# A decoder step on one Trainium2 core: the first loads in smaller pieces for three q products, key pages held back, and every product's three passes 320, 256 and 288 columns wide

## The chip, the cores and the metric

The kernel runs on one core of a Trainium2 chip. The time is device microseconds (us) of one execution, as the median of several runs. The engines are TensorE (PE; its weight loads are listed as PEld), VectorE (DVE), ScalarE (ACT), GpSimd (POOL) and SyncE (SP), which issues most of the DMA transfers from one queue. A name with a q, such as SPq, is an engine's sequencer.

## The reference

One layer of a hybrid decoder is applied to 256 prompt positions and 8 x 4 sample positions. The two groups share all weights, so the kernel treats them as T = 288 columns.

```
h   = RMSNorm(x)                                   # x: 288 x 2048
q, k, v, u, v_g = split(h @ w_in)                  # 5 x 1024 columns
A   = MoBA attention(rope(q), rope(k), v)          # samples also read paged keys and values
B   = gelu(u) * (tril(W_s) @ LN(gelu(v_g)) + b)
mix = (sigmoid(h Wg_a) * (A Wa) + sigmoid(h Wg_b) * (B Wb)) @ w_o
x   = x + RMSNorm(mix)
x   = x + RMSNorm((silu(a1) * g1) @ w_ffn_out)     # a1, g1 = split(RMSNorm(x) @ w_ffn_in)
x   = x + (p @ w_ple) * sigmoid(RMSNorm(x) @ w_ple_gate)
```

The samples' past is 8 x 16 pages of keys and as many of values, 512 KB each, found through a page table. All data are fp32.

## The kernel before

Activations lie transposed, 128 features on the partitions and the 288 positions in a row; 2048 features are 16 such slices, numbered k. The work horse is `product` (L209 to L237): for 256 output columns (two accumulator tiles, t = 0 and 1, one PSUM bank each) it loads weights in pieces of four slices (512 KB, tile `wr`, L218, four buffers). It splits each piece into a rounded part `wh` (ACT, L224) and a remainder `wl` (DVE, L225), three buffers each. The activations have such parts too, side by side in one row of 2 x 288 columns (`hh`, `hl` of `hhl` for the first products; `mhl`, `zhl`, `dhl` later). Three matmuls per slice and tile add up: `wh` times the rounded part (L228), `wh` times the remainder (L229), `wl` times the rounded part (L230).

An argument `wide` shifts columns between the first two: with `wide=32`, L228 takes 320 columns, that is all 288 of the rounded part and the first 32 of the remainder, whose result goes to 32 extra accumulator columns. L229 takes the other 256. After the last slice ACT copies the extra columns out (`rest`, L234), DVE adds them to the first 32 (L235), and only then `done` reads the accumulators. Before the change only the product `f` (w_ffn_out) has `wide=32`; its remainder therefore joins its first pass.

There are 112 products of the other kinds: q, k, v, g and u (four each, from `w_in`), gb and ga (gates), b, a and o (eight each), fa and fg (22 each), pg (eight). Until the last `ga` there are three accumulator banks in pool `acc` (two in `long`, three in `aux`), so a product's second tile takes a bank that the product before it still has to free. From `a` on there are six.

The program's start: ACT issues the load of the gains, SP that of x in four pieces of four slices (576 KB) and the weights of two q products, q0 in `acc` and q1 in `long`. `h_parts` makes `hh` and `hl` of a piece, `squares` its share of the row norm, `r0_of` the factor `r0` from a matmul with ones (`r0p`). Ten matmuls on a constant (`wake`, L168; the trace lists each fp32 matmul of this kind twice) run before any data are there. The constants `cst`, `kcst` (POOL) and `cm` (ACT) are loaded at once, and `page_load` (L554) issues key pages as soon as the table is there, twelve until the buffers are full. A `done` of q multiplies by `r0` and applies the rotation `rope`, which reads `cm`. Then follow k, v, the rest of the first half with the pages' work between the products (`weave`), and from `a` on products alone.

A scheduler with a model of the chip orders the instructions of each engine. `tc.issue_after(i)` tells it that what follows stands after i; on i's own engine that is an order without a wait. SP's DMA transfers go through one queue, and in the trace they land in the order of issue. The transfers of SP and ACT take eight completion semaphores in turn and wait for the one before on theirs, so that at most eight are under way.

Of the kernel before, what the change touches and what calls it, by code (L numbers as in the profile page):

```python
# [19 lines left out]
KD = D // 128  # L20
# [19 lines left out]
GC = 256  # L40

QUADS = NPG // 4
WAKE, WR, BIG, PT, AUX, PB, LEAD, EG, LE, N1, N2, REST = 10, 4, 3, 1, 3, 2, 6, 2, 4, 20, 38, 325.0

# [64 lines left out]
def tile_hybrid_step(ctx: ExitStack, tc: tile.TileContext, a: dict, o: list):  # L109
    nc = tc.nc  # L110
# [34 lines left out]
    ident = cst
# [39 lines left out]

    def h_parts(c):
        for i in range(XK):
            k = c * XK + i
            nc.scalar.activation(hh[:, k], xs[c][:, i], AF.Copy, scale=g_pre[:, k:k + 1])
            nc.vector.scalar_tensor_tensor(hl[:, k], xs[c][:, i], g_pre[:, k:k + 1], hh[:, k], op0=ALU.mult, op1=ALU.subtract)  # L190
# [9 lines left out]
    def r0_of():  # L200
# [5 lines left out]
        rstd_of(r0, r0p, p_x0.tile([128, T], F32, name="r0t"))  # L206


    def product(w, c0, ks, part, done, name, of="acc", wide=0, hold=()):  # L209


        accs = [bank([128, T + wide], f"{name}{t}", of) for t in range(2)]
        n = len(ks)
        for k0 in range(0, n, 4):
            m = min(4, n - k0)
            raw = perm.tile([128, 4, GC], F32, name="wr", bufs=WR)
            r0 = ks[k0] * 128
            nc.sync.dma_start(raw[:, :m], w[r0:r0 + m * 128, c0:c0 + GC].rearrange("(k p) c -> p k c", p=128))  # L218
            wh = perm.tile([128, 4, GC], F32R, name="wh", bufs=3)
# [742 lines left out]
    for half in range(2):  # L962
# [118 lines left out]
```

## Time and profile before

| | |
|---|---|
| three runs | 1820.21, 1820.64 (median), 1822.02 us |
| the profiled execution, its own time | 1820.68 us |
| its span, first to last instruction | 1818.9 us (1.78 us lie around it) |
| PE busy | 1798.5 us, 99% |
| DVE, ACT, POOL busy | 951.9, 769.2, 90.6 us |
| mean granted PE clock | 0.996 of 2.4 GHz |
| HBM read, written | 407.45 MB, 4.85 MB |

PE is busy nearly all the time, but its ends are modelled: matmuls overlap, one starts about 132 ns after the other and is listed with 295 ns. So the time of a stretch of products is read from the starts: its length divided by the number of matmuls in it.

### The profile page before, as it was taken

Reading aid. Unit: us, or ns where it says so; the run is one execution under the profiler, and the core shown is the slowest. Engines: PE = TensorE matmul, PEld = TensorE weight load, DVE = VectorE, ACT = ScalarE, POOL = GpSimd, SP = SyncE. Lnnn points to the kernel's source line nnn. Section 1 sums busy time; section 2 is a strip of 40 time slices with the busy share of each in tenths; the row PEclk is TensorE's granted clock in tenths of the full one; section 3 lists DMA queues with packets and bytes.
Section 4 is the critical chain, followed back from the end, with each engine's and each line's share of the span. In section 5 each row is a group of like instructions: output and inputs, shape, how many; then the busy total and the mean of one; then the engine's idle time right before and its main releaser. Section 6 shows DMA issues by size and latency. Waiting matters only on the chain.

```text
span 1818.9 us, 38387 instructions
## 1 busy us (share of the span) xinstructions
PE 1798.5 (99%) x15818; PEld 1752.1 (96%) x15818; DVE 951.9 (52%) x1363; ACT 769.2 (42%) x1081; POOL 90.6 (5%) x169
## 2 busy tenths in 40 slices
PE   7999999999999999999999999999999999999998
PEld 7999899999999989999999999999999999999998
DVE  6654447544344346544854555434455554444774
ACT  5334465444333344445533333333333333444642
POOL 1010112000000000011000000000000000011000
PEclk9999999999999999999999999999999999999999
DMA  9589999999999995555555555455555555546363
GB/s 345 163 280 367 323 360 337 365 350 359 352 345 368 358 321 201 170 164 161 152 169 166 163 167 169 157 168 165 172 165 172 163 164 170 165 158 195 122 196 112
DMA packets 309136, 414.81 MB, mean 228 GB/s; under 512 B 13120, under 2 KB 273344, under 8 KB 308832
## 3 DMA queue, kind: packets, MB, share of 16 engines
q1 hardware_dynamic: 307728, 409.16, 67.0%
q8 instruction: 124, 2.03, 0.5%
q0 software_dynamic: 944, 2.79, 0.4%
q10 hardware_dynamic: 288, 0.41, 0.1%
q14 instruction: 52, 0.43, 0.1%
HBM read 407.45 MB, written 4.85 MB: 227 GB/s over the span
## 4 chain that ended last, share of the span: by engine, by line
PE 94%; DVE 3%; DMA 1%; SPq 1%; issue 1%; ACT 1%; DVEq 0%; ACTq 0%
PE f L228 6%; PE f L230 5%; PE fg L228 5%; PE fg L230 5%; PE fg L229 5%; PE fa L230 5%; PE fa L228 5%; PE fa L229 5%; PE f L229 5%; PE values L696 3%; PE scores L598 3%; PE gb L228 2%; PE ga L228 2%; PE gb L230 2%; PE o L228 2%; PE o L230 2%
## 5 line engine op out<-in xcount | busy, mean ns | idle before, releaser
L225 DVE TENSOR_TENSOR wl<-wr,wh 128x1024 fp32r<-128x1024 f32 x512 | 618.8, 1209 | 708.2 <-ACT wh L224 704.4
L224 ACT CAST wh<-wr 128x1024 fp32r<-128x1024 f32 x512 | 530.9, 1038 | 881.0 <-PE f L229 140.4
L228 PE MATMUL f<-dhl,wh 128*128 128x320 f32 x704 | 217.1, 308 | 0.0
L229 PE MATMUL fg<-zhl,wh 128*128 128x288 f32 x704 | 208.2, 296 | 0.0
L230 PE MATMUL fa<-zhl,wl 128*128 128x288 f32 x704 | 206.8, 295 | 1.2 <-DVE wl L225 1.2
L229 PE MATMUL fa<-zhl,wh 128*128 128x288 f32 x704 | 207.9, 296 | 0.0
L228 PE MATMUL fg<-zhl,wh 128*128 128x288 f32 x704 | 207.3, 295 | 0.2 <-ACT wh L224 0.2
L230 PE MATMUL fg<-zhl,wl 128*128 128x288 f32 x704 | 207.0, 295 | 0.0
L230 PE MATMUL f<-dhl,wl 128*128 128x288 f32 x704 | 207.0, 294 | 0.0
L228 PE MATMUL fa<-zhl,wh 128*128 128x288 f32 x704 | 206.3, 296 | 0.1
L229 PE MATMUL f<-dhl,wh 128*128 128x256 f32 x704 | 196.6, 279 | 0.0
L230 PEld LDWEIGHTS fa<-zhl,wl 128*128 128x128 f32 x704 | 133.3, 189 | 1.4 <-DVE wl L225 1.4
L230 PEld LDWEIGHTS fg<-zhl,wl 128*128 128x128 f32 x704 | 133.3, 190 | 0.0
L229 PEld LDWEIGHTS f<-dhl,wh 128*128 128x128 f32 x704 | 132.4, 188 | 0.0
L228 PEld LDWEIGHTS fg<-zhl,wh 128*128 128x128 f32 x704 | 132.1, 188 | 0.4 <-ACT wh L224 0.4
L229 PEld LDWEIGHTS fa<-zhl,wh 128*128 128x128 f32 x704 | 132.4, 188 | 0.1
L229 PEld LDWEIGHTS fg<-zhl,wh 128*128 128x128 f32 x704 | 132.3, 188 | 0.0
L228 PEld LDWEIGHTS fa<-zhl,wh 128*128 128x128 f32 x704 | 131.6, 188 | 0.7 <-ACT zhl L937 0.4
L230 PEld LDWEIGHTS f<-dhl,wl 128*128 128x128 f32 x704 | 132.2, 188 | 0.0
L228 PEld LDWEIGHTS f<-dhl,wh 128*128 128x128 f32 x704 | 132.0, 188 | 0.0
L228 PE MATMUL gb<-hhl,wh 128*128 128x288 f32 x256 | 76.7, 300 | 0.0
L228 PE MATMUL ga<-hhl,wh 128*128 128x288 f32 x256 | 76.5, 299 | 0.0
(327 smaller groups left out, 3740.6 us busy)
## 6 DMA issues: line engine op xcount, KB each, us to landing
wr<-in_w_ffn_in SPq DMA_DIRECT2D x176, 512.0 KB, 3.7
kt<-in_cache_k SPq DMA_DIRECT2D x128, 512.0 KB, 7.7
vt<-in_cache_v SPq DMA_DIRECT2D x128, 512.0 KB, 6.6
wr<-in_w_in SPq DMA_DIRECT2D x80, 512.0 KB, 7.2
wr<-in_w_ffn_out SPq DMA_DIRECT2D x80, 512.0 KB, 3.4
wr<-in_w_gate SPq DMA_DIRECT2D x64, 512.0 KB, 7.4
wr<-in_w_o SPq DMA_DIRECT2D x32, 512.0 KB, 3.5
wr<-in_w_ple_gate SPq DMA_DIRECT2D x32, 512.0 KB, 3.5
```

The source lines that it names most:

```text
L224: nc.scalar.copy(wh[:, :m], raw[:, :m])
L225: nc.vector.tensor_tensor(wl[:, :m], raw[:, :m], wh[:, :m], ALU.subtract)
L228: nc.tensor.matmul(accs[t], wh[:, i, c], x[:, :T + wide], start=k == 0, stop=False)
L229: nc.tensor.matmul(accs[t][:, wide:T], wh[:, i, c], x[:, T + wide:], start=False, stop=False)
L230: late["mm"] = nc.tensor.matmul(accs[t][:, :T], wl[:, i, c], x[:, :T], start=False, stop=k == n - 1)
L598: i = nc.tensor.matmul(sp[b][32 * g:32 * g + 32, 4 * n:4 * n + 4], Q[:, h2, g, dq], kt[:, :, c:c + 32], start=h2 == 1 and dq == 0, stop=h2 ...
L696: i = nc.tensor.matmul(oa[b][32 * g:32 * g + 8], w[:, n, 32 * g + 8 * part:32 * g + 8 * part + 8], v[:, :, g], start=first and part == 3, ...
```

## The change

Seven things change. (1) x comes in six pieces: slice 0, slice 1 (issued by ACT), slices 2 and 3, and then three pieces of four slices. (2) Three q products, not two, work on each piece (the third in `aux`), and the weights that meet the small pieces are loaded in pieces of the same slices: six loads of 128 KB, three of 256 KB, and 512 KB from there on. (3) The squares of the last piece and `r0_of` stand behind the matmuls of the second product's last piece. (4) `cst` and `kcst` go through SP behind the twelfth weight load, `cm` through SP behind the fourteenth. (5) The first twelve page loads each stand behind a weight load, the first behind the tenth. (6) `wake` has eight matmuls in place of ten. (7) `wide` is 32 for all products.

```diff
-WAKE, WR, ... = 10, 4, ...
+WAKE, FIRST, WR, ... = 8, 12, 4, ...
...
-    def x_load(c):
-        nc.sync.dma_start(xs[c], a["x"][:, c * XK:c * XK + XK])
+    pieces = [(0, 1), (1, 2), (2, 4)] + [(k, k + XK) for k in range(XK, KD, XK)]
+    def x_load(k0, k1):
+        (nc.scalar if k0 == 1 else nc.sync).dma_start(xs[k0 // XK][:, k0 % XK:k0 % XK + k1 - k0], a["x"][:, k0:k1])
...
-    x_load(0)
+    x_load(*pieces[0])
+    x_load(*pieces[1])
-    nc.gpsimd.dma_start(cst, a["c_perm"][:, :128])
-    nc.gpsimd.dma_start(kcst, a["c_perm"][:, 128:])
...
-    def product(w, c0, ks, part, done, name, of="acc", wide=0, hold=()):
+    def product(w, c0, ks, part, done, name, of="acc", wide=32, cuts=None, hold=()):
-        for k0 in range(0, n, 4):
-            m = min(4, n - k0)
-            raw = perm.tile([128, 4, GC], F32, name="wr", bufs=WR)
+        for k0, k1 in cuts or [(k, min(k + 4, n)) for k in range(0, n, 4)]:
+            m = k1 - k0
+            if cuts and m < 4:
+                raw = p_x0.tile([128, m, GC], F32, name=f"w{m}", bufs=6 // m)
+            else:
+                raw = perm.tile([128, 4, GC], F32, name="wr", bufs=WR)
-            nc.sync.dma_start(raw[:, :m], ...)
+            loads.append(nc.sync.dma_start(raw[:, :m], ...))
...
-    q2 = [q_gen(0), q_gen(1, "long")]
-    for c in range(KD // XK):
-        h_parts(c)
-        for q in q2:
-            next(q)
-        if c + 1 < KD // XK:
-            x_load(c + 1)
-        squares(c)
-    r0_of()
+    q3 = [q_gen(g, of, pieces) for g, of in enumerate(("acc", "long", "aux"))]
+    for i, (k0, k1) in enumerate(pieces):
+        h_parts(k0, k1)
+        for q in q3:
+            if k1 == KD and q is q3[2]:
+                squares(k1 // XK - 1)
+                with tc.issue_after(late["mm"].ins):
+                    r0_of()
+            next(q)
+        if 1 < i + 1 < len(pieces):
+            x_load(*pieces[i + 1])
+        if k1 % XK == 0 and k1 < KD:
+            squares(k1 // XK - 1)
+    with tc.issue_after(loads[11].ins):
+        nc.sync.dma_start(cst, a["c_perm"][:, :128])
+        nc.sync.dma_start(kcst, a["c_perm"][:, 128:])
-    nc.scalar.dma_start(cm, a["c_mix"])
+    with tc.issue_after(loads[13].ins):
+        nc.sync.dma_start(cm, a["c_mix"])
...
+            if len(issued) < FIRST:
+                st.enter_context(tc.issue_after(loads[9 + len(issued)].ins))
...
-    for q in q2 + [q_gen(2), q_gen(3)]:
+    for q in q3 + [q_gen(3)]:
```

The order of the built programs at three places. First PE at the program's start, before; q_116 and q_117 are the two accumulators of the first q product:

```order
L168 MATMUL wake<-ones_d 128x128 x10
L228 MATMUL q_116<-hhl,wh 128x288
L229 MATMUL q_116<-hhl,wh 128x288
L228 MATMUL q_117<-hhl,wh 128x288
L229 MATMUL q_117<-hhl,wh 128x288
L230 MATMUL q_116<-hhl,wl 128x288
L230 MATMUL q_117<-hhl,wl 128x288
```

The same place in the changed program, where q_107 and q_108 belong to the first product, q_121 and q_122 to the second, q_135 and q_136 to the third:

```order
L169 MATMUL wake<-ones_d 128x128 x8
L235 MATMUL q_107<-hhl,wh 128x320
L236 MATMUL q_107<-hhl,wh 128x256
L235 MATMUL q_108<-hhl,wh 128x320
L236 MATMUL q_108<-hhl,wh 128x256
L237 MATMUL q_107<-hhl,wl 128x288
L237 MATMUL q_108<-hhl,wl 128x288
L235 MATMUL q_121<-hhl,wh 128x320
L236 MATMUL q_121<-hhl,wh 128x256
L235 MATMUL q_122<-hhl,wh 128x320
L236 MATMUL q_122<-hhl,wh 128x256
L235 MATMUL q_135<-hhl,wh 128x320
```

The first pass now reads the remainder `hl` too, and after six matmuls on slice 0 the next product's weights for slice 0 are used, where before the first product went on with slices 1 to 3.

Second, SP's queue up to the first key page (`kt`), before:

```order
L137 DMA x_76<-in_x 128x1152
L218 DMA wr<-in_w_in 128x4x256 x2
L137 DMA x_77<-in_x 128x1152
L218 DMA wr<-in_w_in 128x4x256 x2
L137 DMA x_78<-in_x 128x1152
L137 DMA x_79<-in_x 128x1152
L559 TENSOR_LOAD pt_sb
L559 ISA x2
L560 ISA
L560 DMA kt<-in_cache_k 128x1024
L218 DMA wr<-in_w_in 128x4x256
```

In the changed program the queue begins with slice 0 of x, six weight loads of 128 KB, slices 2 and 3 of x and three weight loads of 256 KB. From the first piece of four slices on it reads:

```order
L139 DMA x_77<-in_x 128x1152
L225 DMA wr<-in_w_in 128x4x256 x3
L139 DMA x_78<-in_x 128x1152
L225 DMA wr<-in_w_in 128x4x256
L139 DMA x_79<-in_x 128x1152
L272 DMA cst<-in_c_perm 128x128
L273 DMA kcst<-in_c_perm 128x448
L576 TENSOR_LOAD pt_sb
L576 ISA x2
L577 ISA
L577 DMA kt<-in_cache_k 128x1024
```

Three more pages follow before the next weight load (the fourteenth), and from there on pages and weight loads take turns, one by one. Before, one to four pages stood between two weight loads.

Third, ACT at the program's end, before and after the change; pg_22755 and pg_22756 are the accumulators of the last product:

```order
L1019 ACTIVATE pgt<-pgt 128x288 x2
L224 CAST wh<-wr 128x1024
L1019 ACTIVATE pgt<-pgt 128x288 x2
L1077 UNCONDITIONAL_BRANCH
```

```order
L231 CAST wh<-wr 128x1024
L1036 ACTIVATE pgt<-pgt 128x288
L241 COPY rest<-pg_22755 128x32
L241 COPY rest<-pg_22756 128x32
L1036 ACTIVATE pgt<-pgt 128x288 x2
L1094 UNCONDITIONAL_BRANCH
```

Two copies of 32 columns now stand ahead of the last product's sigmoids, as they do at the end of every product. Where three banks are in use, PE's order mostly has 24 matmuls of a product's first tile ahead of the first of its second tile; before it mostly had 21.

## Rows read from the trace of the kernel before

**Rows 1.** The page, part 1: busy time, share and instructions of each engine.

```profile
PE 1798.5 (99%) x15818; PEld 1752.1 (96%) x15818; DVE 951.9 (52%) x1363; ACT 769.2 (42%) x1081; POOL 90.6 (5%) x169
```

**Rows 2.** Timeline of PE: start and duration (us), instruction, [idle time before it <-releaser].

```profile
1.07 4.63 PE L168 MATMUL wake<-ones_d 128*128 128x128 f32 x20 [1.07 <-DVE eps L160]
9.54 0.61 PE L228 MATMUL q<-hhl,wh 128*128 128x288 f32 x1 [3.84 <-ACT wh L224]
...
42.63 0.40 PE L228 MATMUL q<-hhl,wh 128*128 128x288 f32 x1 [2.50 <-ACT wh L224]
...
45.00 0.85 PE L230 MATMUL q<-hhl,wl 128*128 128x288 f32 x2 [1.58 <-DVE wl L225]
```

**Rows 3.** Busy time in stretches of the start; last: clock, DMA share, GB/s.

```profile
0.00:25.00 25.00, 20.10 (x123) 19.52 (x124) 16.86 (x27) 17.76 (x27) 5.70 (x16) 0.93 0.97 340
25.00:30.00 5.00, 5.00 (x37) 4.79 (x36) 3.22 (x5) 1.56 (x2) 0.00 (x0) 1.00 1.04 389
40.00:45.00 5.00, 0.92 (x5) 0.56 (x4) 4.92 (x10) 2.67 (x3) 0.00 (x0) 0.87 0.86 272
45.00:50.00 5.00, 5.00 (x21) 5.00 (x22) 2.89 (x3) 0.50 (x2) 0.00 (x0) 0.50 0.65 189
0.00:81.19 81.19, 71.16 (x474) 69.05 (x475) 53.42 (x76) 35.09 (x44) 6.43 (x19) 0.94 0.79 267
```

**Rows 4.** The chain that ended last, first 50 us: start, us, what.

```profile
1.21 7.21 DMA wr<-in_w_in
...
23.93 10.81 DMA wr<-in_w_in
...
45.85 0.24 PE q L228
```

**Rows 5.** Timeline of ACT in the same stretch.

```profile
5.52 1.81 ACT L189 ACTIVATE hhl<-x,gains 128x288 fp32r<-128x288 f32 x4 [2.83 <-DMA gains<-in_gains]
...
30.72 1.05 ACT L224 CAST wh<-wr 128x1024 fp32r<-128x1024 f32 x1 [1.66 <-DMA wr<-in_w_in]
```

**Rows 6.** Busy time in stretches: pages' phase, then a, o, fa with fg, f, pg.

```profile
200.00:300.00 100.00, 99.24 (x1190) 90.47 (x1190) 51.76 (x102) 51.91 (x90) 18.44 (x33) 1.00 1.02 366
696.79:748.05 51.26, 51.26 (x384) 51.26 (x385) 35.68 (x60) 22.06 (x32) 0.00 (x0) 1.00 0.64 218
748.05:849.65 101.60, 101.60 (x771) 101.60 (x770) 43.53 (x42) 47.59 (x69) 14.92 (x13) 1.00 0.56 180
899.11:1140.96 241.85, 241.85 (x1827) 241.85 (x1825) 123.42 (x153) 92.73 (x114) 0.00 (x0) 1.00 0.53 166
1140.96:1280.19 139.23, 139.23 (x1059) 139.23 (x1057) 56.70 (x66) 53.85 (x79) 0.00 (x0) 1.00 0.52 165
1738.87:1812.99 74.12, 74.12 (x561) 74.07 (x560) 43.33 (x68) 28.74 (x37) 0.00 (x0) 1.00 0.50 163
```

**Rows 7.** Groups by line and form on ACT and DVE: busy us, mean ns, idle before.

```profile
L224 ACT CAST wh<-wr 128x1024 fp32r<-128x1024 f32 x496 | 520.9, 1051 | 849.5 <-PE fg L229 136.5 <-PE fa L229 127.6 <-PE f L229 108.8
L189 ACT ACTIVATE hhl<-x,gains 128x288 fp32r<-128x288 f32 x16 | 7.2, 524 | 2.8 <-DMA gains<-in_gains 2.8
L234 ACT COPY rest<-f 128x32 f32<-128x32 f32 x32 | 5.6, 175 | 3.6 <-PE f L230 3.6
...
L225 DVE TENSOR_TENSOR wl<-wr,wh 128x1024 fp32r<-128x1024 f32 x496 | 607.7, 1226 | 685.7 <-ACT wh L224 681.9 <-DMA kt<-in_cache_k 3.2 <-PE values L696 0.2
L190 DVE SCALAR_TENSOR_TENSOR hhl<-x,gains,hhl 128x288 fp32r<-128x288 f32 x16 | 7.1, 515 | 0.0
L235 DVE TENSOR_TENSOR f<-f,rest 128x32 f32<-128x32 f32 x32 | 6.2, 193 | 2.1 <-ACT rest L234 2.0
```

**Rows 8.** Timeline of ACT and DVE behind the last `f` product's second tile.

```profile
1699.66 0.19 ACT L234 COPY rest<-f 128x32 f32<-128x32 f32 x1 [0.60 <-PE f L230]
...
1699.87 0.20 DVE L235 TENSOR_TENSOR f<-f,rest 128x32 f32<-128x32 f32 x1
...
1700.11 0.46 DVE L995 TENSOR_TENSOR fo<-fo,f 128x288 f32<-128x288 f32 x1
```

More of the change, by code (lines that the diff above doesn't have):

```diff
@@ L42 @@
 QUADS = NPG // 4
-WAKE, WR, BIG, PT, AUX, PB, LEAD, EG, LE, N1, N2, REST = 10, 4, 3, 1, 3, 2, 6, 2, 4, 20, 38, 325.0
+WAKE, FIRST, WR, BIG, PT, AUX, PB, LEAD, EG, LE, N1, N2, REST = 8, 12, 4, 3, 1, 3, 2, 6, 2, 4, 20, 38, 325.0
 C_ID, C_G, C_OWN, C_L = 0, 128, 256, 256 + TS * NB
@@ L184, in tile_hybrid_step, with h_parts @@
     hh, hl = hhl[:, :, :T], hhl[:, :, T:]
[L186 to L190, printed above, removed]
+    def h_parts(k0, k1):
+        for k in range(k0, k1):
+            x = xs[k // XK][:, k % XK]
+            nc.scalar.activation(hh[:, k], x, AF.Copy, scale=g_pre[:, k:k + 1])
+            nc.vector.scalar_tensor_tensor(hl[:, k], x, g_pre[:, k:k + 1], hh[:, k], op0=ALU.mult, op1=ALU.subtract)
     def squares(c):
@@ L206, in r0_of @@
         rstd_of(r0, r0p, p_x0.tile([128, T], F32, name="r0t"))
-    def product(w, c0, ks, part, done, name, of="acc", wide=0, hold=()):
+    loads = []
+    def product(w, c0, ks, part, done, name, of="acc", wide=32, cuts=None, hold=()):
         accs = [bank([128, T + wide], f"{name}{t}", of) for t in range(2)]
         n = len(ks)
-        for k0 in range(0, n, 4):
-            m = min(4, n - k0)
-            raw = perm.tile([128, 4, GC], F32, name="wr", bufs=WR)
+        for k0, k1 in cuts or [(k, min(k + 4, n)) for k in range(0, n, 4)]:
[4 more added lines that the diff above has]
+                raw = perm.tile([128, 4, GC], F32, name="wr", bufs=WR)
             r0 = ks[k0] * 128
-            nc.sync.dma_start(raw[:, :m], w[r0:r0 + m * 128, c0:c0 + GC].rearrange("(k p) c -> p k c", p=128))
+            loads.append(nc.sync.dma_start(raw[:, :m], w[r0:r0 + m * 128, c0:c0 + GC].rearrange("(k p) c -> p k c", p=128)))
             wh = perm.tile([128, 4, GC], F32R, name="wh", bufs=3)
@@ L245, in tile_hybrid_step, with q_gen @@
     w_gate = a["w_gate"].rearrange("l k c -> (l k) c")
-    def q_gen(g, of="acc"):
-        yield from product(w_in, g * GC, K16, hpart, lambda x: rope(qT[:, 2 * g:2 * g + 2], x), "q", of)
-    q2 = [q_gen(0), q_gen(1, "long")]
-    for c in range(KD // XK):
-        h_parts(c)
-        for q in q2:
-            next(q)
-        if c + 1 < KD // XK:
-            x_load(c + 1)
-        squares(c)
-    r0_of()
+    def q_gen(g, of="acc", cuts=None):
+        yield from product(w_in, g * GC, K16, hpart, lambda x: rope(qT[:, 2 * g:2 * g + 2], x), "q", of, cuts=cuts)
+    q3 = [q_gen(g, of, pieces) for g, of in enumerate(("acc", "long", "aux"))]
[6 more added lines that the diff above has]
+                    r0_of()
+            next(q)
+        if 1 < i + 1 < len(pieces):
[5 more added lines that the diff above has]
+        nc.sync.dma_start(kcst, a["c_perm"][:, 128:])
     end_x0.close()
@@ L1006, in tile_hybrid_step @@
                 le_weights(range(LE, 8))
-            drain(product(w_fo, g * GC, ks, lambda k: dhl[:, k], lambda x, g=g: fo_done(x, g), "f", wide=32))
+            drain(product(w_fo, g * GC, ks, lambda k: dhl[:, k], lambda x, g=g: fo_done(x, g), "f"))
     r4 = norm_gap("fo", range(LE, 8))
```

## The prediction, made before the result was known

> **What bounds the kernel now.** I read the page first: PE is busy 99% of the span [rows 1]. So time can come from two places only: stretches in which PE waits or runs at its lower clock, and the time that one matmul takes. The waits of PE were next, in time order: nearly all lie in the first 50 us [rows 2]. PE does nothing useful until 9.54, then stops at 42.63 (2.50 us) and 45.00 (1.58 us). The reader is to see in [rows 3] what goes with it: the granted clock is 0.93 over the first 25 us and 0.50 from 45 to 50, its lower level of 1.2 GHz; there matmuls start 0.24 us apart [rows 4] where 0.1326 is usual (below).
>
> What ends these waits is DMA. At the start the chain goes through the first weight load, 512 KB that land after 7.21 us at 8.42 [rows 4]; ACT had been ready since 5.52, when the gains landed [rows 5]. Later it goes through a load issued at 23.93 that takes 10.81 us, because key pages lie ahead of it in the queue [rows 4]. The queue itself is full: 340 GB/s over the first 25 us, 389 after [rows 3].
>
> How much the start loses: 81.19 us [rows 3] is a point at which PE has done the four q products (384 matmuls), the four of r0p and 66 of k: 454, the row's 474 less the 20 of wake. At 0.1326 us they are 60.2 us. The loss is 81.19 - 60.2 = 21.0 us.
>
> **The change, part by part.**
>
> *First matmul.* Three things must be there: the gains, slice 0 of x, the first 128 KB of weights. Before, 576 KB of x, 44 KB of gains and other transfers shared the first us, and the gains landed at 5.5. Now 44 + 144 + 128 KB and slice 1 (144 KB) lead. I take 5.0 for gains, x and weights (not earlier than 4.0, not later than 5.5, where the larger pieces had landed). Then ACT makes `hh` (0.52), DVE `hl` (0.52) [rows 7], on which the first pass now depends; the cast of 256 columns beside it is about a quarter of 1.05. First matmul: 6.0 instead of 9.54.
>
> *Work per byte.* For each slice of x three products have 18 matmuls, 2.4 us, for 528 KB of x and weights, about 1.5 us at the rates of [rows 3]. Before it was 12 matmuls per slice. So PE should not run dry in the first slices.
>
> *Clock.* Before, wake ended at 5.7 and PE then stood for 3.84 us [rows 2]; from 9.54 some 14 matmuls ran 0.24 us apart, 1.5 us lost, and from 45 some 23 more, 2.5 us. Now wake ends near 4.8 and work begins at 6.0. I keep 1.0 us of loss (0 to 1.5), and none later, since I see no wait of over a us ahead.
>
> *The fourteenth weight load* is the first behind pages: four of them. Up to its end the queue moves 8.99 MB (gains, all of x, 14 loads, `cst`, `kcst`, four pages). By [rows 3] 8.5 MB are moved at 25 us and the rest by 26.3. What lag follows, an old load shows: ACT starts on it at 30.72, released by DMA [rows 5], with 9.88 MB up to it; these rates give 28.5, so 2.2 us. The fourteenth load then lands near 28.5 and its cast (1.05) ends at 29.5. PE comes to it after 168 matmuls, at 6.0 + 22.3 + 1.0 = 29.3. I take a wait of 0.5 us (0 to 3). After it a load and a page are 1.05 MB, 2.7 us at 389 GB/s, and PE works 24 x 0.1326 = 3.18 us on a load, so the queue gains on PE. `cst`, `kcst` and `cm` add 0.66 MB that was moved before too; their place costs nothing beyond this sum.
>
> *r0 and rope.* Three products now wait for `r0` at once: six multiplications and three rotations on DVE, where there were four and two, among `wl` splits of 1.23 us [rows 7] that PE needs every 3.18 us. `cm` is issued late, behind a load that waits for its buffer, and may come later than `r0`. I add 0.7 us of PE waits (0 to 4).
>
> So the same work is done at 6.0 + 60.2 + 1.0 + 0.5 + 0.7 = 68.4 instead of 81.19: 12.8 us gained. The bounds are 8.5 (first matmul at 7.0, clock 1.5, waits of 2 and 2) and 14.5 (first matmul at 5.0, clock 0.5, waits 0.2 less).
>
> *Does the head start last?* Pages wait for buffers that PE's products free, so the whole later pattern moves along. Where the queue is fullest, 366 GB/s from 200 to 300, PE still works 99.24 of 100 us [rows 6], and 389 has been seen [rows 3].
>
> *The three widths.* Passes of 320, 256 and 288 columns stream 864, as three of 288 do. Whether it pays is read from the only product that has them [rows 6], length by matmuls (those that began before the stretch left out): f 139.23/1056 = 131.85 ns. The others: fa and fg 241.85/1824 = 132.60, pg 74.12/560 = 132.36, o 101.60/768 = 132.29, a 51.26/384 = 133.5. So f is the quickest by 0.4 to 0.75 ns (a apart), but products of one and the same form differ by as much. 9984 matmuls get the new widths: 4224 of fa and fg at 0.75, 768 of o at 0.44, 768 of pg at 0.5, and 4224 others at about 0.6 would give 6.4 us in all. The lower bound is a loss of 2, since operands alone move a matmul by a ns either way. I take 4.0, nearer to the row of f.
>
> The Trainium skill speaks against this gain: "TensorE: Matmul & The Clock Gate", in "Back-to-back issue gap", gives a start-to-start gap of the columns over the clock plus a fixed cost per matmul. By it three passes of equal sum cost the same, and this term is 0. The rows agree on columns and a fixed cost, though with some 12 ns where the page has 2.5; the 0.75 ns of f lie outside the rule.
>
> *Ends of products.* 112 products get two copies (0.175) and two additions (0.193) [rows 7], 39 us on ACT and 43 on DVE in all, on engines that are half idle [rows 1]. They count where nothing covers them. From the copy to the reader of the accumulator is 0.45 us for a tile [rows 8]. This lies bare at the kernel's end (+0.5) and ahead of the row norm behind o (+0.5); that behind f has it already. Elsewhere the next product's first tile covers it. Sum: +1.0, bounds 0.5 and 3.
>
> **Sum**: -12.8 - 4.0 + 1.0 = -15.8. The profiled execution took 1820.68, 0.04 above the median, so both give 1805.
>
> **The rivals.** What a measurement can tell from no change is some 0.2%, 3.6 us.
>
> (A) As summed: 1805, chance 0.53.
>
> (B) The widths give nothing, the start gives all of it: 1820.7 - 12.8 + 1.0 = 1809. For it: forms alike differ by as much as f does from them. Against: f is below each of them, and keeps it over 1056 matmuls. Chance 0.24. It is what the skill's rule would make of the change.
>
> (C) The start gives much less. Small pieces keep the queue emptier: with few transfers under way it moved 189 GB/s [rows 3]. Were the first 2.1 MB moved at this rate, not at 380, they would take 11.1 us, not 5.5; PE would run dry for 5.6 us and lose some 2.5 more at its lower clock, as from 45 us on: 1805 + 8 = 1813. Against it: six pieces are issued before anything has landed. Chance 0.10.
>
> (D) The head start is given back: if the queue sets the pace of the pages' phase, PE meets it there and waits 13 us longer, and the widths gain only behind it, about 2.5 us: 1820.7 - 2.5 + 1.0 = 1819, no change. Against: 99.24 of 100 us busy [rows 6]. Chance 0.05.
>
> (E) Slower: the three-bank boundaries. Some 41 products start while the product before still holds a bank. Its release now takes a copy, an addition and the reader, and the copy and the addition may each stand behind a cast (1.05) and a split (1.23) [rows 7]: with 0.45 for the reader some 3.1 us in all, against 24 matmuls or 3.18 us of cover. One more cast ahead would make PE wait about 0.6 us each: 41 x 0.6 = 25, so 1830. It decides from 15.8/41 = 0.39 us per product on. Against it: most orders leave 24 matmuls as cover. Chance 0.08.
>
> **The numbers.** Faster by over 0.2% are A, B and C, and a mild form of E: 0.88. Same 0.05, slower 0.07. The range goes from A with the start at its upper bound and the widths at theirs (1820.7 - 14.5 - 6.4 + 0.5 = 1800), widened by a us for what a shifted order may add, to C: 1799 to 1814. D and E lie outside.
>
> **What the profile would show.** Right: first product matmul near 6 us, no PE wait of over 1.5 us in the first 80, qrp and the first k products some 12 us earlier, lower clock nowhere behind 15 us; fa, fg, o, pg at about 131.9 ns per matmul; the pages' phase as busy as before; the end longer by half a us. Wrong: a first matmul later than 8, a wait at the fourteenth load (it would be released by ACT `wh` behind DMA), waits of L235 on bank releases by DVE between 80 and 700 us, pitches of 132.3 or more in fa, or key pages on the chain.

## The result

| | median (lowest to highest) | ratio to before, 95% interval |
|---|---|---|
| before | 1820.3 us (1818.87 to 1822.02, 5 runs) | |
| changed | 1800.88 us (1799.44 to 1801.96, 5 runs) | 0.9891, 0.9877 to 0.9906 |

The changed kernel is faster by 19.4 us, or 1.1%. Forecast were 1805 and 1799 to 1814. The profiled execution took 1801.96 us, of which the span is 1800.2. Direction and size came out; the two large terms of the sum did not. Their errors pull in opposite directions, so that the total comes this close is in part luck.

The page's first part, which answers to [rows 1]: PE is busy 15.0 us less than before.

```profile
PE 1783.5 (99%) x15814; PEld 1739.2 (97%) x15814; DVE 987.4 (55%) x1593; ACT 797.8 (44%) x1309; POOL 84.6 (5%) x167
```

The timeline of PE in the start, beside [rows 2]: start and duration in us, the instruction, in brackets the idle time before it and what ended it.

```profile
3.79 1.06 PE L169 MATMUL wake<-ones_d 128*128 128x128 f32 x4
4.59 0.61 PE L235 MATMUL q<-hhl,wh 128*128 128x320 f32 x1
...
10.46 0.41 PE L235 MATMUL q<-hhl,wh 128*128 128x320 f32 x1 [0.50 <-DVE hhl L191]
...
16.72 0.53 PE L237 MATMUL q<-hhl,wl 128*128 128x288 f32 x2 [0.46 <-DVE wl L232]
...
31.16 0.42 PE L235 MATMUL q<-hhl,wh 128*128 128x320 f32 x1 [2.04 <-ACT wh L231]
...
32.42 0.67 PE L237 MATMUL q<-hhl,wl 128*128 128x288 f32 x2 [0.47 <-DVE wl L232]
```

Windows of the start, beside [rows 3] (busy us of PE, PEld, DVE, ACT and POOL with counts; last the granted clock, the DMA share, GB/s). 71.68 is where the 66th k matmul starts; before, it started at 81.06, and was done 0.13 us later, at the 81.19 of [rows 3].

```profile
0.00:25.00 25.00, 22.98 (x154) 22.34 (x155) 17.23 (x32) 19.28 (x34) 4.55 (x14) 1.00 0.94 320
25.00:30.00 5.00, 4.12 (x32) 3.90 (x30) 4.25 (x6) 1.64 (x2) 0.00 (x0) 1.00 1.05 379
30.00:35.00 5.00, 3.38 (x15) 3.15 (x16) 2.30 (x2) 2.09 (x2) 0.00 (x0) 0.77 1.06 375
35.00:40.00 5.00, 5.00 (x36) 5.00 (x35) 1.90 (x3) 2.10 (x2) 0.00 (x0) 0.89 1.07 379
...
0.00:71.68 71.68, 67.15 (x469) 65.85 (x470) 51.40 (x85) 36.99 (x58) 4.55 (x14) 0.98 0.88 300
```

The reader is to see three things. The first product matmul now follows `wake` without a gap (4.59 for 9.54), and the first 25 us have a granted clock of 1.00. Then PE waits 2.04 us at 31.16, for the cast of the fourteenth weight load. Behind this wait the clock falls for the only time in the start: 0.77 and 0.89 over ten us, so 0.23 x 5 + 0.11 x 5 = 1.7 us are lost at the lower level, 1.2 GHz. The chain (start, us, what) shows the load behind it, beside [rows 4]:

```profile
21.16 8.82 DMA wr<-in_w_in
30.06 1.05 ACT wh L231
```

The products' stretches, beside [rows 6]: a, o, fa with fg, f, pg.

```profile
684.45:735.08 50.63, 50.63 (x387) 50.63 (x385) 39.59 (x76) 24.95 (x48) 0.00 (x0) 1.00 0.66 223
735.08:836.34 101.26, 101.26 (x771) 101.26 (x770) 46.00 (x58) 49.55 (x85) 13.95 (x13) 1.00 0.56 180
886.39:1125.53 239.14, 239.14 (x1826) 239.14 (x1825) 128.87 (x192) 97.79 (x153) 0.00 (x0) 1.00 0.54 168
1125.53:1264.77 139.24, 139.24 (x1058) 139.24 (x1057) 57.16 (x68) 53.85 (x80) 0.00 (x0) 1.00 0.52 165
1720.19:1793.74 73.55, 73.55 (x561) 73.46 (x560) 45.36 (x81) 30.69 (x52) 0.00 (x0) 1.00 0.51 164
```

Length by matmuls, as before: fa and fg 239.14/1824 = 131.11 ns (132.60), a 50.63/384 = 131.85 (133.5), o 101.26/768 = 131.85 (132.29), pg 73.55/560 = 131.3 (132.36), f 131.86 (131.85). So fa, fg and pg fell below f, which was the best row before.

Where the 18.7 us of span came from, by when the same matmul starts: 9.4 are gained at the 66th matmul of k, 12.3 at a's first, 13.3 behind o, 15.4 at f's first, 19.2 at the last of pg, 18.7 at the end. Two places give time back: the norms ahead of fa (1.35 us) and ahead of pg (0.56), where fa's and pg's first pass of 320 columns now needs 32 columns of the remainder `zl`, and the kernel's end (0.53). The first is seen in the waits of PE (us in total, times, longest):

```profile
PE q L235 <- ACT wh L231: 2.0, 1, 2.0
PE fa L235 <- DVE zhl L955: 1.5, 1, 1.5
PE pg L235 <- DVE zhl L955: 1.5, 1, 1.5
```

Before, pg waited 0.9 at this place for ACT's half of `zhl`.

### The profile page after: what moved, and what is told of

It is laid out like the page before. It is cut to its first block, busy times and chain, and to the rows that moved or that the text cites. A ratio compares the mean times of both kernels' runs of the same rounds, so it can differ in the third digit from the quotient of the medians.

```text
span 1800.2 us, 38851 instructions
## 1 busy us (share of the span) xinstructions
PE 1783.5 (99%) x15814; PEld 1739.2 (97%) x15814; DVE 987.4 (55%) x1593; ACT 797.8 (44%) x1309; POOL 84.6 (5%) x167
## 4 chain that ended last, share of the span: by engine, by line
PE 93%; DMA 2%; DVE 2%; SPq 1%; issue 1%; ACT 0%; ACTq 0%; DVEq 0%
PE fg L235 6%; PE f L235 6%; PE fa L235 6%; PE f L237 5%; PE fg L237 5%; PE fa L237 5%; PE f L236 5%; PE fg L236 5%; PE fa L236 4%; PE values L713 3%; PE scores L615 3%; PE gb L235 2%; PE o L235 2%; PE gb L237 2%; PE o L237 2%; PE pg L235 2%
## 5 line engine op out<-in xcount | busy, mean ns | idle before, releaser
L232 DVE TENSOR_TENSOR wl<-wr,wh 128x1024 fp32r<-128x1024 f32 (+1 forms) x509 | 614.8, 1209 | 636.9 <-ACT wh L231 630.6
L231 ACT CAST wh<-wr 128x1024 fp32r<-128x1024 f32 (+1 forms) x509 | 526.3, 1035 | 647.0 <-issue 174.0
L235 PE MATMUL fa<-zhl,wh 128*128 128x320 f32 x704 | 219.1, 312 | 1.5 <-DVE zhl L955 1.5
L235 PE MATMUL fg<-zhl,wh 128*128 128x320 f32 x704 | 219.2, 312 | 0.0
L235 PE MATMUL f<-dhl,wh 128*128 128x320 f32 x704 | 217.4, 309 | 0.0
L237 PE MATMUL f<-dhl,wl 128*128 128x288 f32 x704 | 207.2, 294 | 0.0
L237 PE MATMUL fa<-zhl,wl 128*128 128x288 f32 x704 | 204.5, 292 | 1.2 <-DVE wl L232 1.2
L237 PE MATMUL fg<-zhl,wl 128*128 128x288 f32 x704 | 204.7, 291 | 0.0
L236 PE MATMUL fa<-zhl,wh 128*128 128x256 f32 x704 | 196.9, 280 | 0.0
L236 PE MATMUL fg<-zhl,wh 128*128 128x256 f32 x704 | 196.7, 279 | 0.0
L235 PEld LDWEIGHTS fa<-zhl,wh 128*128 128x128 f32 x704 | 132.2, 188 | 1.8 <-DVE zhl L955 1.7
L237 PEld LDWEIGHTS fa<-zhl,wl 128*128 128x128 f32 x704 | 131.9, 188 | 1.5 <-DVE wl L232 1.5
L236 PEld LDWEIGHTS f<-dhl,wh 128*128 128x128 f32 x704 | 132.6, 188 | 0.0
L237 PEld LDWEIGHTS f<-dhl,wl 128*128 128x128 f32 x704 | 132.3, 188 | 0.0
L235 PEld LDWEIGHTS fg<-zhl,wh 128*128 128x128 f32 x704 | 132.2, 188 | 0.1
L236 PEld LDWEIGHTS fa<-zhl,wh 128*128 128x128 f32 x704 | 132.2, 188 | 0.1
L236 PEld LDWEIGHTS fg<-zhl,wh 128*128 128x128 f32 x704 | 132.2, 188 | 0.0
L235 PEld LDWEIGHTS f<-dhl,wh 128*128 128x128 f32 x704 | 132.2, 188 | 0.0
L237 PEld LDWEIGHTS fg<-zhl,wl 128*128 128x128 f32 x704 | 132.0, 188 | 0.0
L235 PE MATMUL pg<-zhl,wh 128*128 128x320 f32 x256 | 79.5, 312 | 1.5 <-DVE zhl L955 1.5
L235 PE MATMUL gb<-hhl,wh 128*128 128x320 f32 x256 | 80.2, 314 | 0.0
```

What stands on the lines that cost most here:

```text
L231: nc.scalar.copy(wh[:, :m], raw[:, :m])
L232: nc.vector.tensor_tensor(wl[:, :m], raw[:, :m], wh[:, :m], ALU.subtract)
L235: nc.tensor.matmul(accs[t], wh[:, i, c], x[:, :T + wide], start=k == 0, stop=False)
L236: nc.tensor.matmul(accs[t][:, wide:T], wh[:, i, c], x[:, T + wide:], start=False, stop=False)
L237: late["mm"] = nc.tensor.matmul(accs[t][:, :T], wl[:, i, c], x[:, :T], start=False, stop=k == n - 1)
```

## The experiments

Twelve kernels ran. Beside each stands the time of the kernel before that was measured along with it.

| kernel | median, us | before, us | ratio, 95% interval |
|---|---|---|---|
| w288_all: start only | 1807.63 | 1819.28 | 0.9937, 0.992 to 0.9953 |
| w320_only: widths only | 1811.51 | 1819.28 | 0.9956, 0.994 to 0.9973 |
| pages_later | 1798.32 | 1819.28 | 0.9887, 0.987 to 0.9903 |
| pages_free | 1805.32 | 1819.28 | 0.9931, 0.9914 to 0.9947 |
| fourpieces | 1803.8 | 1821.12 | 0.9906, 0.989 to 0.9923 |
| two_q | 1803.6 | 1821.12 | 0.9905, 0.9888 to 0.9921 |
| apart | 1808.65 | 1821.12 | 0.993, 0.9914 to 0.9947 |
| w64_all | 1847.51 | 1821.12 | 1.0143, 1.0126 to 1.016 |
| w16_all | 1816.34 | 1820.29 | 0.9975, 0.9963 to 0.9986 |
| w48_all | 1815.04 | 1820.29 | 0.9966, 0.9952 to 0.9981 |
| placed | 1793.1 | 1819.71 | 0.9852, 0.9835 to 0.9868 |
| placed0 | 1805.75 | 1819.83 | 0.9922, 0.9908 to 0.9935 |

### The two halves of the change

w288_all is the changed kernel with three equal passes in all products but f; w320_only is the kernel before with the three widths in all.

```diff
-    def product(w, c0, ks, part, done, name, of="acc", wide=32, cuts=None, hold=()):
+    def product(w, c0, ks, part, done, name, of="acc", wide=0, cuts=None, hold=()):
...
-... lambda x, g=g: fo_done(x, g), "f"))
+... lambda x, g=g: fo_done(x, g), "f", wide=32))
```

> The changed kernel with three passes of 288 columns in every product but f, the new start kept. Theory 1 (the start gives 9.4 us, the widths 10 us less 1 us at the ends): about 1810 us, fa and fg back at 132.6 ns per matmul, the 66th matmul of k still near 72 us. Rival (the widths give the 4 us of the prediction, the rest came from moved tiles or another order): about 1804 us, with fa below 132.6 ns.

The other, from the kernel before:

```diff
-    def product(w, c0, ks, part, done, name, of="acc", wide=0, hold=()):
+    def product(w, c0, ks, part, done, name, of="acc", wide=32, hold=()):
```

> The kernel before with 320, 256 and 288 columns in all products, its old start kept. Theory 1: about 1811 us, fa near 131.1 ns per matmul, start as before (66th matmul of k near 81 us). Rival (the widths alone give 4 us less 1): about 1817 us.

Measured: the start alone is worth 1819.28 - 1807.63 = 11.65 us, the widths alone 1819.28 - 1811.51 = 7.8. The sum is 19.4, the whole change, so no help or hindrance between the halves is seen. The windows of fa with fg, first with the start only, then with the widths only:

```profile
888.29:1129.46 241.17, 241.17 (x1826) 241.17 (x1825) 123.84 (x155) 92.69 (x114) 0.00 (x0) 1.00 0.54 166
```

```profile
896.09:1135.24 239.15, 239.15 (x1827) 239.15 (x1826) 128.51 (x191) 97.69 (x153) 0.00 (x0) 1.00 0.55 168
```

These are 132.22 and 131.11 ns: the widths do it, whatever the start. (The start's half too takes 0.38 ns off fa's 132.60, with no width changed; over 4224 matmuls that is 1.6 of its 11.65 us. In the compiled programs `zhl` has the same address in both, the tiles of the weights have not: `wh` begins at 22,048 in the kernel before and at 5,664 here. What makes the 0.38 was not tried.) The start only has the wait (1.6 us) and the fall of the clock, too (0.78 from 30 to 35), so neither comes from the widths.

### The start: what the fourteenth load waits for

pages_later holds the first key page back to the sixteenth weight load. pages_free holds none back: its first six pages stand where they did, but the next six stand earlier, two ahead of one weight load and four ahead of the next.

```diff
-                st.enter_context(tc.issue_after(loads[9 + len(issued)].ins))
+                st.enter_context(tc.issue_after(loads[15 + len(issued)].ins))
```

> The changed kernel with its first page behind the sixteenth weight load and not the tenth, pages still one per load. Theory 2 (the wait of 2.04 us at the fourteenth load, the 0.6 us behind it and the half-clock stretch that follows, some 2.2 us, come from the four pages ahead of that load): 1796 us, no PE wait of over 1 us before 60 us, clock full throughout. Rival (the same transfers only wait elsewhere: later loads, cm or the first scores are late instead): 1800 to 1802 us with a new wait of 2 us or more before 100 us.

```diff
-WAKE, FIRST, WR, ... = 8, 12, 4, ...
+WAKE, FIRST, WR, ... = 8, 0, 4, ...
```

> The changed kernel without the pacing of pages; six of the first pages stand as in the changed kernel, but then two and four pages stand ahead of a weight load. Theory 2: these four extra pages, 1.3 us each, make a load some 4 us late, so 1804 to 1807 us with a PE wait of 2 us or more near 45 us. Rival (pacing is hidden by the buffers already filled): 1801 us.

Windows of pages_later; 67.44 is where the 66th k matmul starts (71.68 in the changed kernel):

```profile
25.00:30.00 5.00, 5.00 (x40) 5.00 (x40) 5.00 (x6) 3.98 (x5) 0.00 (x0) 1.00 1.06 367
30.00:35.00 5.00, 5.00 (x40) 5.00 (x40) 3.48 (x4) 1.59 (x2) 0.00 (x0) 1.00 1.03 351
0.00:67.44 67.44, 65.37 (x470) 64.37 (x470) 49.82 (x83) 37.18 (x58) 4.55 (x14) 1.00 0.94 319
```

The waits and the fall of the clock are gone and 4.2 us are won at this point: 2.04 + 0.47 us of waits and 1.7 at the lower clock are 4.2. At the end 3.8 us of span are left (1800.2 to 1796.4), 2.6 in the medians; the intervals of the two ratios overlap, so it is the trace that shows this gain and not the time. So the pages ahead of that load cause its wait. The fall of the clock goes with the wait: from 30 to 35 us the clock is 0.67 to 0.87 in the seven runs that have it (the changed kernel, w288_all, pages_free, w16_all, w48_all, w64_all, apart) and 1.00 in pages_later, fourpieces, placed and placed0, which have none, and in two_q, where PE waits 0.92 there. A wait alone is not enough, though: behind 1.52 us at 48.38 in pages_free the clock stays at 1.00. Waits of PE in pages_free from 20 to 60 us:

```profile
PE q L235 <- ACT wh L231: 2.6, 2, 1.5
PE q L237 <- DVE wl L232: 1.7, 2, 1.2
```

They are 4.3 us in all for 2.5 in the changed kernel. So the pacing helps; it still lets the pages in too early.

fourpieces takes x and the first weights in four pieces again; two_q takes two q products along with x. In both, the loads behind which `cst`, `kcst`, `cm` and the first pages stand are counted anew (not shown in the cuts), so that these follow the same slices as in the changed kernel.

```diff
-    pieces = [(0, 1), (1, 2), (2, 4)] + [(k, k + XK) for k in range(XK, KD, XK)]
+    pieces = [(k, k + XK) for k in range(0, KD, XK)]
```

> x and the first weights in four pieces of four slices again, all else as in the changed kernel (three q products, key pages and constants behind the same bytes). Theory 1, small pieces are worth what they bring the first matmul forward: it comes at 7.5 to 9 us in place of 4.6, PE stands idle behind wake and loses 1.5 us at the lower clock; 1800.9 + 4 + 1.5 = about 1806. Theory 2, most of it is given back at the first weight load behind key pages: a PE that comes there 5 us later finds it landed, so the wait of 2.0, the 0.6 around it and the 2.2 us at the lower clock behind it go; 1806.4 - 4.8 = about 1801.6, hardly different from the changed kernel.

```diff
-    q3 = [q_gen(g, of, pieces) for g, of in enumerate(("acc", "long", "aux"))]
+    q3 = [q_gen(g, of, pieces) for g, of in enumerate(("acc", "long"))]
...
-    for q in q3 + [q_gen(3)]:
+    for q in q3 + [q_gen(2), q_gen(3)]:
```

> Two q products go along with x instead of three, the other two follow; six pieces, key pages one behind each weight load from the same slice on. Theory 1, the third product matters because it gives PE more work per byte: from the fourth slice on a piece of four slices is 2.69 MB (x, two weight loads, two pages) for 48 matmuls, 6.35 us, 423 GB/s, where three products have 3.7 MB for 72 matmuls, 390 GB/s; the queue has moved 389 at most, so PE's lead shrinks, the wait at the first loads behind pages grows from 2.0 to 4 or 5 us with more of it at the lower clock: 1804 to 1807. Theory 2, the third product does nothing for the time, the pages' pace does: 1800 to 1802.

The timeline of PE in fourpieces has one wait after `wake`. Its clock is 0.50 from 10 to 15 us, and 1.00 from 30 to 35:

```profile
10.85 0.63 PE L235 MATMUL q<-hhl,wh 128*128 128x320 f32 x1 [6.00 <-ACT wh L231]
```

```profile
10.00:15.00 5.00, 4.15 (x16) 3.87 (x17) 4.17 (x4) 4.76 (x7) 0.00 (x0) 0.50 1.06 392
...
30.00:35.00 5.00, 5.00 (x40) 5.00 (x39) 2.45 (x2) 1.82 (x2) 0.00 (x0) 1.00 1.05 377
```

Its first product matmul comes 6.26 us later than the changed kernel's, its 66th of k only 1.8 us later (73.47). By that point PE has met none of the later waits, so 4.5 of the 6.26 us that small pieces bring at 4.59 are given back. Most of that is the wait at the key pages with the clock behind it, 4.2 us by pages_later; the rest is a balance of the waits between the small pieces and of what fourpieces itself loses at the lower clock. That is theory 2's mechanism. The time alone decides less: 1803.8 lies 2.2 us above theory 2's 1801.6 and as much below theory 1's 1806.

two_q has no fall of the clock. Its waits up to 60 us:

```profile
PE q L237 <- DVE wl L232: 1.6, 3, 0.9
PE q L235 <- ACT wh L231: 1.4, 2, 1.0
PE q L235 <- DVE hhl L191: 0.4, 1, 0.4
```

Theory 1 wanted 4 or 5 us at the first loads behind pages; here PE waits 0.92 there, 1.0 at the longest anywhere, and the 66th k matmul comes 1.1 us earlier than with three products. The median is 0.0014 of the time above the changed kernel's, within the intervals. So nothing shows that the third product gains anything; I had its worth per byte wrong.

### The widths: why some products gain 1.5 ns and some none

w64_all, w16_all and w48_all change one number, apart gives fa, fg and pg equal widths again and moves their remainders.

```diff
-    def product(w, c0, ks, part, done, name, of="acc", wide=32, cuts=None, hold=()):
+    def product(w, c0, ks, part, done, name, of="acc", wide=64, cuts=None, hold=()):
```

> All products' passes take 352, 224 and 288 columns; the sum of columns is that of 320, 256 and 288. What is asked: why the new widths save 1.1 to 1.5 ns per matmul for some operands. Theory W, the unequal widths themselves save (a longer first pass hides something that the next needs): a second step of 32 columns saves something again or at least keeps the saving, so fa and fg stay at 131.1 ns start to start or below, f at 131.85 or below, and the time is 1794 to 1801. Theory A, what counts is where the second pass's operand begins: 1,280 bytes behind the first operand with 320 columns, a multiple of 256; with 352 columns it is 1,408, no multiple of 256, as the 1,152 of equal widths are. Then fa and fg go back to about 132.2, o to 132.2, a to 133.4, and the time is about 1807.6, that of the changed kernel with equal widths.

```diff
-    zhl = p_z.tile([128, KD, 2 * T], F32R, name="zhl")
-    zh, zl = zhl[:, :, :T], zhl[:, :, T:]
+    zhl = p_z.tile([128, 2, KD, T], F32R, name="zhl")
+    zh, zl = zhl[:, 0], zhl[:, 1]
...
-..., done_g, "fg")]
+..., done_g, "fg", wide=0)]
```

> The changed kernel, but fa, fg and pg have three equal passes of 288, and their operand's remainders lie apart from its main parts, 18,432 bytes behind them, a multiple of 256. All others keep 320, 256 and 288. Theory A (the place of the second operand counts): fa, fg and pg keep 131.1 ns at equal widths, the time is 1800 to 1801 (the end is 0.5 us shorter without the copy and the addition). Theory W (the unequal widths count): they go back to 132.2; 4,992 matmuls by 1.1 ns are 5.5 us, the time is about 1806.

Windows of w64_all (a, fa with fg, f), then of apart (fa with fg):

```profile
697.73:749.78 52.05, 52.05 (x387) 52.05 (x385) 40.12 (x76) 25.34 (x49) 0.00 (x0) 1.00 0.63 215
904.72:1151.98 247.26, 247.26 (x1826) 247.26 (x1825) 129.79 (x191) 98.75 (x153) 0.00 (x0) 1.00 0.53 162
1151.98:1295.12 143.14, 143.14 (x1059) 143.14 (x1058) 57.74 (x68) 54.35 (x81) 0.00 (x0) 1.00 0.50 161
```

```profile
887.45:1128.62 241.17, 241.17 (x1827) 241.17 (x1825) 123.39 (x153) 92.54 (x114) 0.00 (x0) 1.00 0.54 166
```

With 352, 224 and 288 columns a, fa with fg, and f each take 135.5 ns (52.05/384, 247.26/1824, 143.14/1056): 3.7 to 4.4 ns more, in passes of the same sum. Both theories had forecast 1794 to 1808 and fell; the time is 1847.5. Three rows of its timeline show where it goes:

```profile
1000.04 0.26 PE L236 MATMUL fa<-zhl,wh 128*128 128x224 f32 x1
1000.15 0.31 PE L237 MATMUL fa<-zhl,wl 128*128 128x288 f32 x1
1000.29 0.32 PE L235 MATMUL fa<-zhl,wh 128*128 128x352 f32 x1
```

The 288 columns of L237 now take 0.14 us from start to start; in the changed kernel 0.12 to 0.13. apart is 132.22 ns, as equal widths side by side were: an operand 18,432 bytes behind (a multiple of 256) does not help, so theory A found no support. (It is no clean test: apart also halves the step from slice to slice to 1,152 bytes, so every other slice of `zhl` lies 128 bytes further from a multiple of 256 than before.) It is the widths, but not the more the better. Two sizes between:

> All products' passes take 304, 272 and 288 columns. So far, three passes of one set in fa take 397 ns with 288, 288 and 288 columns, 393.5 with 320, 256 and 288, and 407 with 352, 224 and 288. Theory W1, each column moved from the second pass to the first saves a little until the second pass is too short to cover what the next one needs (with 224 its successor of 288 columns took 142 ns in place of 128 to 131): half the step saves about half, fa and fg at 131.7 ns, the time is about 1804. Theory W2, it is a property of the lengths 320 and 256 themselves, and half the step saves nothing or costs: fa and fg at 132.2 or more, 1807 or more.

> All products' passes take 336, 240 and 288 columns. Theory W1 as for 304, 272 and 288: the loss of 352, 224 and 288 begins where the second pass gets too short; if it grows evenly from 256 down to 224, fa's three passes take about 400 ns and the time is about 1824 (half of the 46 us); if the step down is at 240 or under, the saving goes on and the time is 1795 to 1801. Theory W2 (320 and 256 are good lengths by themselves): 336 and 240 are no better than 288, 1807 or more.

Windows of a and of fa with fg, for w16_all (304, 272, 288) and w48_all (336, 240, 288):

```profile
687.88:739.06 51.18, 51.18 (x387) 51.18 (x385) 39.47 (x76) 24.73 (x48) 0.00 (x0) 1.00 0.65 220
890.88:1132.73 241.85, 241.85 (x1826) 241.85 (x1825) 128.26 (x192) 97.39 (x153) 0.00 (x0) 1.00 0.54 166
```

```profile
688.18:738.82 50.64, 50.64 (x387) 50.64 (x386) 39.87 (x76) 25.14 (x48) 0.00 (x0) 1.00 0.66 223
891.45:1132.62 241.17, 241.17 (x1826) 241.17 (x1825) 129.50 (x192) 98.31 (x153) 0.00 (x0) 1.00 0.54 166
```

fa with fg take 132.59 and 132.22 ns, a 133.3 and 131.87. So theory W1 (a smooth saving up to a limit) fell, and what W2 forecast came: of these widths 320 and 256 alone bring fa to 131.11. Why is not shown. 320 is also the only first width of the four whose second pass begins a multiple of 256 bytes behind the first (1,280; with 304, 336 and 352 it is 1,216, 1,344 and 1,408), and no run tells the lengths from this place. The same few values come back in kernel after kernel: 131.11, 131.85, 132.22, 132.59, 133.33, 135.5. (The times of these two kernels say less: the size of `rest` moves `hhl`, `mhl` and `dhl` by 128 bytes, and f rose to 133.33 in both; `zhl`, the operand of fa and fg, stays. What that means came out next.)

The compiled program of the changed kernel gives the byte addresses of the operands, and what lies behind the last multiple of 256:

```
hhl  46880   32    (q, k, v, g, u, gb, ga)
bhl 209760   96    (b)
ahl 172896   96    (a)
mhl  65312   32    (o)
zhl 141536  224    (fa, fg, pg)
dhl  65312   32    (f)
```

In the stretches read above, the operand at 224 takes 131.11, those at 32 (o, f) and 96 (a) take 131.85. placed moves all but `bhl` to 224, on top of pages_later; placed0 moves the same ones to a multiple of 256.

```diff
+    p_h.tile([128, 48], F32, name="pad")
     hhl = p_h.tile([128, KD, 2 * T], F32R, name="hhl")
...
     ahl = p_ab.tile([128, H, 2 * T], F32R, name="ahl")
+    p_ab.tile([128, 32], F32, name="pad2")
...
+    p_m.tile([128, 48], F32, name="pad3")
     mhl = p_m.tile([128, KD, 2 * T], F32R, name="mhl")
...
+    p_f.tile([128, 48], F32, name="pad4")
     dhl = p_f.tile([128, HT, 2 * T], F32R, name="dhl")
```

> The kernel with key pages from the sixteenth load on (1798.3), in which the operands of q, k, v, u, gb, ga, a, o and f begin 192 or 128 bytes further on (or back) in SBUF, so that they lie as that of fa, fg and pg does (224 bytes behind a multiple of 256; before 32 or 96); the operand of b stays where it was (96), fa, fg and pg too. Passes of 320, 256 and 288 columns everywhere. Theory P, where the operand lies decides why fa, fg and pg take 131.1 ns start to start and f, o and a 131.85: now f, o and a take 131.1 too, b stays; some 8,800 matmuls by 0.74 ns are 6.5 us, the time is about 1792. Theory Q, it has another cause: f, o and a stay at 131.85 and the time at 1798, within 1 us.

placed0 has 56, 24, 56 and 56 for 48, 32, 48 and 48.

> As the kernel with the placed operands (1793.1), but those of q, k, v, u, gb, ga, a, o and f begin at a multiple of 256 bytes in place of 224 behind one; those of fa, fg and pg (224) and of b (96) stay. Theory P1, only where the 256 bytes are crossed counts, and a multiple is at least as good as 224: f, o and a take 131.1 ns or less, the time is 1793 or less. Theory P2, 224 is a good place among several bad ones: f, o and a go back to 131.85 or more, the time is 1798 or more.

Windows of placed (a, o, fa with fg, f):

```profile
678.49:728.84 50.35, 50.35 (x386) 50.35 (x385) 39.58 (x76) 24.92 (x48) 0.00 (x0) 1.00 0.66 224
728.84:829.54 100.70, 100.70 (x771) 100.70 (x769) 46.29 (x58) 49.46 (x85) 14.00 (x13) 1.00 0.56 181
879.61:1118.76 239.15, 239.15 (x1826) 239.15 (x1825) 128.44 (x191) 97.61 (x153) 0.00 (x0) 1.00 0.54 168
1118.76:1257.21 138.45, 138.45 (x1058) 138.45 (x1057) 57.12 (x68) 53.80 (x80) 0.00 (x0) 1.00 0.52 166
```

And of placed0 (a, o, fa with fg, f):

```profile
684.42:735.62 51.20, 51.20 (x387) 51.20 (x386) 39.60 (x76) 24.91 (x48) 0.00 (x0) 1.00 0.64 220
735.62:838.02 102.40, 102.40 (x771) 102.40 (x769) 46.34 (x58) 49.44 (x85) 13.95 (x13) 1.00 0.56 178
888.04:1127.18 239.14, 239.14 (x1826) 239.14 (x1825) 128.49 (x191) 97.67 (x153) 0.00 (x0) 1.00 0.54 168
1127.18:1267.97 140.79, 140.79 (x1058) 140.79 (x1057) 57.21 (x68) 53.78 (x80) 0.00 (x0) 1.00 0.51 164
```

Moved to 224, a, o and f take 131.1 ns each (50.35/384, 100.70/768, 138.45/1056); moved to 0 they take 133.3, while fa, which stayed, takes 131.11 in both. For these three theory P holds (5.2 us of its 6.5 came), and of the last two P2: 32 bytes more cost 2.2 ns per matmul, 12.7 us in the time. In pages_later, placed and placed0 every engine has the same instructions in the same order; what differs are addresses, those of the operands and, by the same pads, of the key and value tiles and some others. placed, at 1793.1, is faster than both kernels: its interval lies below that of the changed one.

But the place does not fix the pitch alone. P had said that b stays, and `bhl` does lie at 209,760 in both programs; yet 42 matmuls in a row, of its last unbroken stretch, take 131 ns each in pages_later and 133.3 in placed:

```profile
541.47:546.97 5.50, 5.50 (x44) 5.50 (x43) 3.24 (x4) 1.80 (x2) 1.88 (x5) 1.00 0.91 264
```

```profile
540.14:545.74 5.60, 5.60 (x44) 5.60 (x43) 2.83 (x4) 1.78 (x2) 1.62 (x6) 1.00 0.89 277
```

And in two_q, a takes 131.1 ns (378 matmuls, the first and the last three left out) with `ahl` at 96, where the changed kernel's a takes 131.85:

```profile
684.63:734.19 49.56, 49.56 (x380) 49.56 (x379) 38.80 (x74) 23.70 (x45) 0.00 (x0) 1.00 0.66 219
```

What else decides, such as what PE ran just before or the places of the other tiles, was not tried.

## Why the prediction came out as it did

The sum was -12.8 (start) - 4.0 (widths) + 1.0 (ends). Measured: the start won 9.4 us at the 66th k matmul (11.65 in the whole time of w288_all, with the 1.6 of fa and fg), and the widths, net of the ends, 7 to 8. The start fell short by 3.4 and the widths came out 4 to 5 above; that they nearly cancel is luck.

- **First matmul.** Forecast 6.0 (5.0 to 7.0), measured 4.59. ACT starts on `hhl` at 3.36, released by the gains, where it had waited for them until 5.52 [rows 5]. The step "I take 5.0 for gains, x and weights" was 1.6 us too late, and from there to the first matmul took 1.23 for 1.0.
- **Clock.** Right for the first 25 us by the record, 1.00, though the first three q matmuls start 0.41, 0.21 and 0.21 us apart. "And none later, since I see no wait of over a us ahead" was wrong: the 2.04 us at 31.16 cost 1.7 more at 1.2 GHz. pages_later takes away both.
- **Fourteenth load.** The place and the mechanism were right, the size was not: 2.04 and 0.47 for 0.5. PE came at 31.16 - 2.04 = 29.12, as forecast (29.3); the load landed at 21.16 + 8.82 = 29.98, not at 28.5. The step that was off is "8.5 MB are moved at 25 us", taken from the larger pieces of before [rows 3]. The small ones moved 320 GB/s, 8.0 MB; 0.5 MB at 379 are 1.3 us.
- **r0 and rope.** 0.7 us were set aside; no row shows a wait for them. The four matmuls of r0p start 0.24 us apart, and the sum had them at 0.13. Bare waits instead were 0.50 and 0.46, on `hhl` and `wl` between the first pieces.
- The sum for this point is then 4.59 + 60.2 + 3.5 of waits + 1.7 of clock = 70.0, for 71.81. The rest, 1.8, lies in the starts: about 0.4 at the first three matmuls, 0.5 at r0p and behind it, and 1.1 because the four waits cost more from start to start than the idle time listed for them (28.82 to 31.16 is 2.34 where 0.13 is usual, for a listed 2.04), less 0.2 for matmuls that follow a little closer than 0.1326.
- **Head start kept.** Yes: 9.4 at k, 12.3 at a. D is out.
- **Widths.** Forecast 4.0 (-2 to 6.4), "nearer to the row of f". This step was off: f's 131.85 was no floor. placed brought f itself to 131.11 with its operand at 224, where `zhl` lies from the beginning. Above the upper bound, too: fa and fg alone give (241.85 - 239.14)/1824 x 4224 = 6.3 us, pg 0.8, a 0.6, o 0.3. That "products of one and the same form differ by as much" was a hint that I read as scatter. Whether places make these differences with three equal passes no run shows: fa went from 132.60 to 132.22 in w288_all with `zhl` where it was.
- **B**, no gain from the widths, is out: w288_all is 6.75 us slower than the change, by the medians. The Trainium skill's rule in "TensorE: Matmul & The Clock Gate", "Back-to-back issue gap" (columns over the clock and a constant, there for an isolated matmul) would give one time for all these sums of 864 columns; measured in a dense stream were 131.1 to 135.5 ns per matmul, so here the measurement decides.
- **Ends.** 0.5 at the kernel's end, as forecast. The norms cost 1.35 and 0.56 where 0.5 was taken for one, because the 320-column pass reads `zl`, which I had named for the first product (`hl`) and not for fa and pg. In all 2.4, within 0.5 to 3.
- **C and E** did not come: no dry stretch in the small pieces beyond 0.5 us, no waits of L235 on bank releases between 80 and 700 us.

What stays open: by what way the place of an operand and the lengths of passes move the pitch, and what else does (b and two_q's a change with their operand in place). With 320, 256 and 288 columns only places of 0, 32, 96 and 224 were read, and whether the weights' places matter too was not tried.

## What to carry to other kernels

Where PE is busy 99% of the time, read the pitch of each product apart, and where products of one form differ, look at where their operands lie in SBUF before taking the difference for scatter: pads of 128 and 192 bytes were worth 5 us here (1798.32 to 1793.1). Measure it each time, since one place can show two pitches. A first matmul brought forward is paid out only if the transfer that PE meets next is earlier too; find the next late load and what was put ahead of it. A pass that is made longer also reads more of its operand, and may wait for what it did not need before.

## What the hardware showed that was not expected

- The time per matmul moves with the operand's byte address. Passes of 320, 256 and 288 fp32r columns took 133.3 ns at 0 behind a multiple of 256 (a, o, f), 131.85 at 32 (o, f), 131.1 at 224 (a, o, f, fa with fg), each over 384 matmuls or more, at a granted clock of 1.00. The address is not all: at 96, a took 131.85 in the changed kernel and 131.1 in two_q.
- It does not grow evenly with the widths either. At 224 (fa with fg): 132.2 to 132.6 with 288, 288, 288; 132.59 with 304, 272; 131.11 with 320, 256; 132.22 with 336, 240; 135.5 with 352, 224. The place of the second pass changes along with the widths.
- Small first pieces fill the queue a little less: 320 GB/s over the first 25 us for 340 [rows 3]; fourpieces, with larger ones, has 338. I had reckoned with the old rate.
